# A hybrid attention layer on one core: modulation weights in long rows, and inverse roots spread by an identity matmul

## The chip, the cores and the metric

The kernel runs on one core of one Trainium2 chip. The metric is device time in microseconds: the median of several runs of the compiled program. The profile is of one further execution. Engines are named as the profile names them: PE (TensorE matmuls), PEld (its weight loads), DVE (VectorE), ACT (ScalarE), POOL (GpSimd), SP (SyncE, which issues the loads and stores).

## The reference

One layer of a diffusion backbone, depth 1, model width 1024, 1024 latent tokens and 256 context tokens, in float32. What matters here, cut:

```python
sh_a, sc_a, g_a, sh_f, sc_f, g_f = split(silu(c) @ w_ada + b_ada, 6)      # latent tokens
csh_a, csc_a, ...                = split(silu(c_ctx) @ w_ada + b_ada, 6)  # context tokens
h = rmsnorm(x) * (1 + sc_a) + sh_a
qa, ka, va, cq, ckv, krope = split(h @ w_in)          # 512, 512, 512, 256, 128, 32 columns
qb  = rmsnorm(cq, q_a_norm) @ w_q_up ; kvb = rmsnorm(ckv, kv_a_norm) @ w_kv_up
oa  = softmax(q1 k1) v - lam * softmax(q2 k2) v       # 4 differential heads of 2 x 64
oa  = rmsnorm(oa, diff_subln) * (1 - lam_init)
ob  = softmax(qb kb) vb                               # 8 latent heads
new = x + g_a * (concat(oa, ob) @ w_out)
h   = rmsnorm(new) * (1 + sc_f) + sh_f
out = rmsnorm(new + g_f * ((silu(h @ w_gate) * (h @ w_up)) @ w_ffn_out), final_norm)
```

An rmsnorm divides each token by the root of the mean of its squares. The modulation vectors (sh, sc, g) are products of one vector, silu(c) or silu(c_ctx), with columns of `w_ada` (1024 x 6144).

## The kernel before

Activations lie transposed: model columns on the 128 partitions, in 8 chunks k of 128, tokens along the free axis in slices of 512, 512 and 256 (`SLICES`). To keep float32 accuracy, most operands are split in a high and a low part of the rounded type fp32r (`split`: ACT copies the high part, DVE or POOL subtracts it), and a product is three matmuls, high by high, high by low, low by high. Plain f32 matmuls are used for small sums. A plain f32 matmul shows in the trace as two matmul instructions (two passes).

**First stage** (lines 446 to 621, order written out by hand for PE, ACT, DVE and POOL; SP issues loads in program order and waits there for a buffer to come free). The tokens x come in 8 loads of 640 KB, rows of 5 KB. ACT squares them, DVE adds the squares up (L541, L543), and `column_sums` (L416) gives the sum of each token with f32 matmuls of two columns. `inverse_rms` (L420, L421) makes the inverse root, tokens on the partitions. To multiply it into x it must lie along the free axis on every partition: `spread` (L423) writes the diagonal matrices identity times inverse, 128 x 128 for each 128 tokens, on DVE for the first slice and on POOL for the others (L426), and multiplies them by a matrix of ones (L427); ACT copies the result to `rstd`.

The modulation of chunk k needs two blocks of `w_ada` (1024 x 128 each, shift and scale), loaded by `load_ada` (L466, two loads of 512 KB in rows of 512 bytes; the tag `wa` has three buffers), split (`split_ada`; low parts on POOL and DVE, L479), multiplied by silu(c) and silu(c_ctx), both split too, four columns (`ada_part`, L506: 16 matmuls of 256 columns), copied to a row (`ada_row`, L510), turned to columns (L515) and added to the bias (`ada_columns`, L517). `modulate` (L524, L525, L528) scales, shifts and splits x to `hH` and `hL`. `group` (L600) then multiplies chunk k into seven PSUM banks for three blocks of `w_in` (cq, ckv): 14 matmuls for the high part, 7 for the low part. The products of chunk k + 1's modulation stand between them.

**Projections** (to about 345 us): the other blocks of `w_in`, rope, the low-rank norms (`low_stats`, `low_diag` L743, `low_norm` L759) and stores to DRAM; between them POOL sums the modulation rows of the later vectors (`mod_row`, L675 to L681). The first to execute are the key columns (`wk2`, L834).

**Attention** (to about 800 us): a list of operations, `attention_graph`, with engine, duration, dependencies and priority; a planner, `schedule`, orders them before the program is built. The norm of the differential heads is in it: `square`, `sums`, `mean`, `root`, `inverse_root`, `diagonal` (POOL, L1196), `spread` (PE, L1200), `apply` (DVE).

**Output projection, second norm, feed-forward, final norm**: `stat` (L1304) sums squares and writes the diagonals on DVE (L1316), `spread_stat` (L1319) multiplies them by ones (L1321). This occurs for each half of the tokens after its output projection, and in three parts at the end.

## Time and profile before

| | |
|---|---|
| runs, median of 3 | 1575.68 us (1570.89 to 1576.01) |
| profiled execution, its own time | 1571.2 us |
| its span, first to last instruction | 1569.3 us |
| PE busy, share of the span | 96% |
| DVE, ACT, POOL | 72%, 48%, 50% |

Busy time of PE is pipelined, a matmul's duration holds its way through the array, so two that follow each other overlap; what one costs in a stream is the distance between starts. Times in a trace are microseconds from the start of the span.

### The profile page before, as it was taken

What the parts mean: (1) busy time and instruction counts of PE and PEld (TensorE: products, weight loads), DVE (VectorE), ACT (ScalarE), POOL (GpSimd) and SP (SyncE); (2) the same over time, 40 slices, a digit from 0 to 9 for tenths busy, and PEclk for the clock granted to TensorE, in tenths of its full rate; (3) what the DMA queues carried; (4) which work ended last, traced back from release to release, by engine and by line L of the source; (5) the groups of instructions that cost most, each with busy time, mean ns of one, the idle gap of its engine ahead of it and who ended that gap; (6) DMA issues with size and microseconds to landing.
All of it is one profiled execution on the core that took longest, in us unless ns stands there. A gap on an engine that the chain in (4) does not pass through costs nothing.

```text
span 1569.3 us, 20682 instructions
## 1 busy us (share of the span) xinstructions
PE 1499.1 (96%) x7323; PEld 1210.4 (77%) x7323; DVE 1123.8 (72%) x1630; ACT 752.5 (48%) x1184; POOL 787.0 (50%) x547
## 2 busy tenths in 40 slices
PE   4899999989999999999999989999999999999997
PEld 2577888866777878888878767888888888888876
DVE  5758565569999879999854697655555555899883
ACT  5443321157777766777753454333333333444451
POOL 2437245526777847756511565755544441484221
PEclk8899999999999999999999989999999999999999
DMA  8426988596344434533146302322222224975633
GB/s 262 140 80 215 318 293 241 179 272 164 91 104 110 121 108 128 121 115 98 58 117 186 128 27 81 121 81 81 81 81 81 81 81 136 358 271 180 208 101 108
DMA packets 153922, 227.69 MB, mean 145 GB/s; under 512 B 11215, under 2 KB 80859, under 8 KB 153819
## 3 DMA queue, kind: packets, MB, share of 16 engines
q1 hardware_dynamic: 153547, 226.11, 46.7%
q8 instruction: 58, 0.95, 0.2%
q14 instruction: 45, 0.37, 0.1%
q10 hardware_dynamic: 272, 0.26, 0.0%
HBM read 172.53 MB, written 53.81 MB: 144 GB/s over the span
## 4 chain that ended last, share of the span: by engine, by line
PE 70%; DVE 10%; DMA 6%; POOL 5%; issue 3%; ACT 3%; SPq 1%; DVEq 0%; ACTq 0%; POOLq 0%
PE mm L1427 25%; PE mm L1715 10%; PE S L1056 10%; PE T L1118 6%; PE acc L1135 4%; PE acc L1140 3%; PE mm L1355 3%; PE mm L410 2%; PE ps L1355 1%; DMA wa<-in_w_ada_dram 1%; PE mm L600 1%; POOL sh L645 1%; POOL macc L681 1%; PE S L1355 1%; POOL e L1104 1%
## 5 line engine op out<-in xcount | busy, mean ns | idle before, releaser
L1056 PE MATMUL S<-kt,qt 128*128 128x512 f32 (+1 forms) x768 | 197.9, 362 | 10.5 <-ACT e L1090 8.7
L1090 ACT ACTIVATE e<-S,nm 128x1280 f32<-128x1280 f32 x128 | 170.3, 1331 | 46.4 <-DVE nm L1076 37.9
L1715 PE MATMUL mm<-block 128*128 128x512 f32 x792 | 179.7, 389 | 0.0
L1122 ACT ACTIVATE ph<-T 128x512 fp32r<-128x512 f32 x240 | 140.3, 597 | 81.9 <-PE T L1118 77.7
L1715 PEld LDWEIGHTS mm<-block 128*128 128x128 f32 x792 | 148.7, 188 | 30.8
L1072 DVE TENSOR_REDUCE nm<-S 128x1 f32<-128x1024 f32 x128 | 156.2, 1220 | 22.5 <-PE S L1056 21.1
L1126 DVE TENSOR_TENSOR pl<-T,ph 128x512 fp32r<-128x512 f32 x240 | 160.0, 682 | 15.8 <-ACT ph L1122 15.0
L1056 PEld LDWEIGHTS S<-kt,qt 128*128 128x128 f32 x768 | 131.8, 189 | 39.1 <-ACT e L1090 15.1
L1118 PE MATMUL T<-ident,e 128*128 128x128 f32 x960 | 140.4, 274 | 3.1 <-DVE pl L1126 1.7
L1110 POOL TENSOR_SCALAR e<-e,ls 128x1280 f32<-128x1280 f32 x64 | 88.0, 1376 | 102.6 <-DVE ls L1107 71.5
L1118 PEld LDWEIGHTS T<-ident,e 128*128 128x128 f32 x960 | 114.0, 141 | 32.1 <-DVE pl L1126 6.4
L1135 PE MATMUL acc<-ph,vt 128*128 128x512 f32 x320 | 120.9, 418 | 1.1 <-DVE otmp L1156 1.0
L1427 PE MATMUL mm<-fresh,wh 128*128 128x512 f32 x352 | 114.8, 406 | 3.4 <-DVE fresh L1580 3.3
L1427 PE MATMUL mm<-block,wh 128*128 128x512 f32 x352 | 112.2, 400 | 0.0
L1140 PE MATMUL acc<-pl,vt 128*128 128x512 f32 x240 | 104.6, 436 | 0.0
L1532 POOL TENSOR_TENSOR hd<-acc,v 128x512 f32<-128x512 f32 x22 | 29.7, 1349 | 149.4 <-DVE acc L1528 137.8
L344 ACT ACTIVATE wh<-wf 128x1024 fp32r<-128x1024 f32 (+1 forms) x51 | 52.2, 1025 | 103.4 <-issue 68.2
L1300 POOL TENSOR_TENSOR acc<-acc,sq 128x512 f32<-128x512 f32 x23 | 34.3, 1489 | 124.6 <-ACT sq L1298 124.0
L1104 POOL TENSOR_TENSOR e<-e,e 128x1280 f32<-128x1280 f32 x32 | 94.2, 2944 | 2.7
L410 PE MATMUL mm<-hH,wh 128*128 128x512 f32 (+1 forms) x256 | 95.2, 372 | 0.0
L410 PE MATMUL mm<-hH,wl 128*128 128x512 f32 (+1 forms) x256 | 94.0, 367 | 0.0
L410 PE MATMUL mm<-hL,wh 128*128 128x512 f32 (+1 forms) x256 | 93.8, 367 | 0.0
(357 smaller groups left out, 3613.3 us busy)
## 6 DMA issues: line engine op xcount, KB each, us to landing
wf<-in_w_ffn_in_dram SPq DMA_DIRECT2D x44, 512.0 KB, 3.7
hidD<-hd SPq DMA_DIRECT2D x44, 256.0 KB, 2.1
wh<-in_w_ffn_out_dram SPq DMA_DIRECT2D x21, 512.0 KB, 5.3
wl<-hidD SPq DMA_DIRECT2D x17, 512.0 KB, 5.7
wa<-in_w_ada_dram SPq DMA_DIRECT2D x16, 512.0 KB, 4.0
wa<-in_w_ada_dram SPq DMA_DIRECT2D x32, 256.0 KB, 3.7
qt<-QB SPq DMA_DIRECT2D x32, 256.0 KB, 4.7
qt<-QA SPq DMA_DIRECT2D x32, 256.0 KB, 4.9
```

The lines of the kernel that those rows point to most:

```text
L410: PE.matmul(ps, a(k), b(k), start=start and i == 0, stop=stop and i == n - 1)
L1056: m = PE.matmul(S[:, c0:c0 + w], q, k[:, k0:k0 + w], start=s == 0, stop=s == len(job) - 1)
L1072: on_banks(DVE.tensor_reduce(self.stats(n)[0][:, i:i + 1], sl, AX.X, ALU.max, negate=True), BANKS[i], DVE)
L1090: m = ACT.activation(e, S[:, i * NT:(i + 1) * NT], AF.Exp, bias=self.s[n][0][:, i:i + 1], accum_out=total)
L1104: POOL.tensor_tensor(self.e[n, 0], self.e[n, 0], self.e[n, 1], ALU.add)
L1118: PE.transpose(self.T[c][:, b * P:(b + 1) * P], e[:, kc * P:(kc + 1) * P], ident)
L1122: ACT.activation(self.ph[c], self.T[c], AF.Copy)
L1126: DVE.tensor_tensor(self.pl[c], self.T[c], f32(self.ph[c]), ALU.subtract)
L1135: PE.matmul(self.acc[u, qh, j], vt[:, kc, v], self.ph[c], start=kc == 0 and i == 0, stop=False)
L1140: PE.matmul(self.acc[u, qh, j], self.kv[u][1][:, kc, v], self.pl[c], start=False, stop=kc == 9)
L1427: PE.matmul(ps, a[:, k, :], b, start=k == 0 and i == 0, stop=k == 3 and i == 2)
L1715: PE.matmul(ps[d], w[:, sl], x[:, t0:t0 + n], start=first and c == 0 and i == 0, stop=c == NH - 1 and i == 2, skip_group_check=not first)
```

## The change

It has four parts.

1. *Layout.* The first 2048 columns of `w_ada` become an input of their own, `w_first`, so arranged that each load of `load_ada` reads rows of 4 KB; `w_ada` keeps the rest. `w_in` and `w_out` are stored by blocks of 128 columns, which also gives rows of 4 KB.
2. *Order and buffers of the first stage.* Chunk 0's weights are loaded after two blocks of x, two of the three `w_in` blocks between the others; chunk 2's weights and the key columns are loaded later. High and low parts of the modulation weights get a buffer for each half. All low parts are made on DVE. The loop over chunks is rearranged: modulation of chunk k + 1 and weights of chunk k + 2 are worked on beside chunk k's products.
3. *Three chunks unsplit.* The weights of chunks 0, 1 and 2 aren't split; `ada_whole` multiplies them in f32, 16 matmuls of 128 columns. For the other five, `ada_parts` has 32 matmuls of 128 columns in the place of 16 of 256.
4. *Spreading.* In all norms the diagonals go: `spread` multiplies, for each 128 tokens, the column of inverses, repeated 128 times by a stride of zero, by the identity. In attention the operation `diagonal` leaves the planner's list.

```diff
     def spread(h, qh, root):
-        d = op("Pool", 1.4, [root] + spreads[-1:], "diagonal", h, qh)
-        s = after("T", op("PE", 0.86, [d] + T[-2], "spread", h, qh, kind="diagonal"))
+        s = after("T", op("PE", 0.86, [root] + T[-2], "spread", h, qh, kind="diagonal"))
         a = op("DVE", 0.66, [s], "apply", h, qh, kind="diagonal")
         T.append([a])
         spreads.append(s)
...
-    def spread(ps, rs, dg, n, eng):
+    def spread(ps, rs, n):
 
         for t in range(n // P):
-            eng.tensor_scalar(dg[:, t * P:(t + 1) * P], ident, rs[:, t:t + 1], 1.0, ALU.mult, ALU.mult)
-        PE.matmul(ps[:, :n], ones, dg[:, :n], start=True, stop=True)
+            PE.matmul(ps[:, t * P:(t + 1) * P], rs[:, t:t + 1].to_broadcast([P, P]), ident, start=True, stop=True)
 
     def win_cols(c0, m):
-        return w_in.rearrange("(k p) c -> p k c", p=P)[:, :, c0:c0 + m]
+
+        return w_in[:, c0 * KD:(c0 + m) * KD].rearrange("p (k c) -> p k c", k=KD)
...
-    for k in range(KD):
+
+    def part_tile(tag):
+        return sp.tile([P, KD, P], F32R, tag=tag, name=tag, bufs=4)
+
+    def room(tag, n):
+        return f32(part_tile(tag)).rearrange("p a b -> p (a b)")[:, 0:n]
+
+    pieces = slice(0, 512), slice(512, NT)
+    acc = [room("wal", 512), room("wal", 768)]
+    sqs = [room("wah", 512), room("wah", 768)]
+    small = room("wal", 512)
+    smalls = small[0:60, 384:512]
+    lp = small[:, 0:256].rearrange("p (a b) -> p a b", b=64)
+    pr = small[:, 256:384].rearrange("p (a b) -> p a b", b=64)
+
+    def load_x(k):
         dma(x[:, k, :], xT[k * P:(k + 1) * P, :])
-        if k == 1:
-            dma(smalls, vecs.rearrange("(c p) -> c p", p=P))
-            dma(lp, diff_lambda.rearrange("a b -> (a b)").partition_broadcast(P))
 
     def load_ada(k):
 
         was = []
         for i in range(2):
             was.append(sp.tile([P, KD, P], F32, tag="wa", name="wa", bufs=3))
-            dma(was[i], w_ada.rearrange("(r p) c -> p r c", p=P)[:, :, i * D + k * P:i * D + (k + 1) * P])
+            dma(was[i].rearrange("p r c -> p (r c)"), w_first[k][:, i * D:(i + 1) * D])
         return was
...
-    def split_ada(wa, eng, eng2=None, between=None):
-        wah, wal = ada_tiles()
+    def split_ada(wa, between=None):
+        wah, wal = ([part_tile(tag) for i in range(2)] for tag in ("wah", "wal"))
         for i in range(2):
-            ACT.activation(wah[:, i], wa[i], AF.Copy)
+            ACT.activation(wah[i], wa[i], AF.Copy)
         for i in range(2):
-            if i and between:
+            DVE.tensor_tensor(wal[i], wa[i], f32(wah[i]), ALU.subtract)
+            if i == 0 and between:
                 between()
-            (i and eng2 or eng).tensor_tensor(wal[:, i], wa[i], f32(wah[:, i]), ALU.subtract)
         return wah, wal
...
     st.enter_context(tc.manual_schedule(engines=ENGINES))
+    load_x(0)
+    load_x(1)
     was = [load_ada(0)]
-    mixw = [fetch_w(mix_cols(i), P) for i in range(2)]
+    dma(smalls, vecs.rearrange("(c p) -> c p", p=P))
+    dma(lp, diff_lambda.rearrange("a b -> (a b)").partition_broadcast(P))
+    mixw = []
+    for k in range(2, KD, 2):
+        load_x(k)
+        load_x(k + 1)
+        if k < KD - 2:
+            mixw.append(fetch_w(mix_cols(k // 2 - 1), P))
     was.append(load_ada(1))
     wkr = sp.tile([P, KD, 32], F32, name="wkr")
-    dma(wkr, win_cols(1920, 32))
-    was.append(load_ada(2))
...
+    def ada_whole(k):
+
+        for i in range(2):
+            for r in range(KD):
+                PE.matmul(adp[0:2, i * P:(i + 1) * P], cv[:, r, :], was[k][i][:, r, :], start=r == 0, stop=r == KD - 1)
...
+    def ada_parts(w):
+
+        for i in range(2):
+            for n, p in enumerate(w):
+                for r in range(KD):
+                    PE.matmul(adp[0:4, i * P:(i + 1) * P], c4[:, r, :], p[i][:, r, :], start=r + n == 0, stop=r == KD - 1 and n == 1)
+
+    def ada_row(m):
+        row = sp.tile([4, 256], F32, tag="row", name="row", bufs=1)[0:m]
+        ACT.activation(row, adp[0:m, 0:256], AF.Copy)
+        return row, sel if m == 4 else ident[0:2, 0:2]
+
+    def ada_turn(row, sel):
         for i in range(2):
             PE.matmul(adp[:, 256 + 2 * i:258 + 2 * i], row[:, i * P:(i + 1) * P], sel, start=True, stop=True)
+
+    def ada_columns(k):
         for i in range(2):
             DVE.tensor_scalar(modA[:, 8 * i + k, :], adp[:, 256 + 2 * i:258 + 2 * i], bT[:, 8 * i + k:8 * i + k + 1],
                               float(i), ALU.add, ALU.add)
...
-    def modulate(k):
+    def scale(k):
         for j, (t0, n) in ((0, (0, 512)), (0, (512, 512)), (1, (1024, 256))):
             sl = slice(t0, t0 + n)
             sh, sc, t = modA[:, k, j:j + 1], modA[:, 8 + k, j:j + 1], x[:, k, sl]
             DVE.scalar_tensor_tensor(t, t, sc, rstd[:, sl], ALU.mult, ALU.mult)
             ACT.activation(hH[:, k, sl], t, AF.Identity, bias=sh)
+
+    def shift_low(k):
...
     for k in range(KD):
-        for sq, sl in zip(sqs, halves):
-            sq = sq if k else acc[:, sl]
+        for sq, to, sl in zip(sqs, acc, pieces):
+            sq = sq if k else to
             ACT.activation(sq, x[:, k, sl], AF.Square)
             if k:
-                DVE.tensor_tensor(acc[:, sl], acc[:, sl], sq, ALU.add)
+                DVE.tensor_tensor(to, to, sq, ALU.add)
...
+        if k == 3:
+            ada_whole(0)
+        if k == 6:
+            row = ada_row(2)
+        if k in (5, 6):
+            split(*mixw[k - 5])
         if k >= KD - 3:
 
             for t0 in (0, 512):
                 PE.matmul(warm, ones, x[:, k, t0:t0 + 512], start=True, stop=True)
-    column_sums(msp, acc, NT)
-    adp = mm_tile()
-    wads = [ada_tiles()]
-    wah, wal = wads[0]
-    for i in range(2):
-        ACT.activation(wah[:, i], was[0][i], AF.Copy)
-    ACT.activation(mixw[0][0], mixw[0][2], AF.Copy)
+    ada_turn(*row)
+    rstd = sp.tile([P, NT], F32, name="rstd")
     rsc = sp.tile([P, 10], F32, name="rsc")
-    DVE.tensor_tensor(wal[:, 0], was[0][0], f32(wah[:, 0]), ALU.subtract)
+    msp = mm_tile()
+    column_sums(msp, acc[0], 512)
+    column_sums(msp[:, 8:], acc[1], 768)
     inverse_rms(rsc, msp[:, 0:20], D)
-    ACT.activation(mixw[1][0], mixw[1][2], AF.Copy)
-    ada_part(wads[0], 0)
-    rstd = sp.tile([P, NT], F32, name="rstd")
+    ada_columns(0)
     for i, (t0, n) in enumerate(SLICES):
         rb = mm_tile()
-        spread(rb, rsc[:, t0 // P:], dg[:, t0:t0 + n], n, POOL if i else DVE)
-        if i == 0:
-            DVE.tensor_tensor(wal[:, 1], was[0][1], f32(wah[:, 1]), ALU.subtract)
-            for w in mixw:
-                DVE.tensor_tensor(w[1], w[2], f32(w[0]), ALU.subtract)
+        spread(rb, rsc[:, t0 // P:], n)
         ACT.activation(rstd[:, t0:t0 + n], rb[:, :n], AF.Copy)
-    ada_part(wads[0], 1)
-
 
...
-    ada_columns(0, ada_row())
-    wads.append(split_ada(was[1], POOL, DVE, lambda: modulate(0)))
+    scale(0)
     mixw.append(fetch_w(mix_cols(2), P))
+    was.append(load_ada(2))
+    dma(wkr, win_cols(1920, 32))
+    ada_whole(1)
+    row = ada_row(2)
+    shift_low(0)
     split(*mixw[2])
-    wads.append(split_ada(was[2], POOL, DVE))
+    wads = {}
     wk2 = const.tile([P, KD, 64], F32R, name="wk2")
 
-    def group(k, part):
-        for ps, (b, i) in zip(lows, low):
+    def group(k, part, which=low):
+        for ps, (b, i) in zip(lows[low.index(which[0]):], which):
             t0, n = SLICES[i]
             x_ = h_parts(t0, n)[part]
             for w in range(2 - part):
                 PE.matmul(ps[:, :n], mixw[b][w][:, k, :], x_(k), start=k == 0 and part == 0 and w == 0,
                           stop=k == KD - 1 and part == 1)
 
+    group(0, 0, low[:5])
+    ada_turn(*row)
     for k in range(KD):
-        if k == 0:
-            group(0, 0)
-        if k + 1 < KD:
-            for i in range(2):
-                ada_part(wads[k + 1], i)
-            row = ada_row()
         if k + 3 < KD:
             was.append(load_ada(k + 3))
-            wads.append(split_ada(was[k + 3], POOL, DVE if k % 2 else None))
-        if k == 3:
+        if k + 1 < KD:
+            ada_columns(k + 1)
+            scale(k + 1)
+        low_part = (lambda: shift_low(k + 1)) if k + 1 < KD else None
+        if k + 3 < KD:
+            wads[k + 3] = split_ada(was[k + 3], low_part)
+        elif low_part:
+            low_part()
+        if k == 4:
             split(wk2[:, :, 0:32], wk2[:, :, 32:64], wkr)
-        group(k, 1 if k == 0 else 0)
-        if k + 1 < KD:
-            ada_columns(k + 1, row)
-            modulate(k + 1)
         if k:
-            group(k, 1)
+            group(k, 0)
+        else:
+            group(0, 1, low[:5])
+            group(0, 0, low[5:])
+        if k + 2 < KD:
+            if k:
+                ada_parts(wads[k + 2])
+            else:
+                ada_whole(2)
+            row = ada_row(4 if k else 2)
+        group(k, 1, low if k else low[5:])
+        if k + 2 < KD:
+            ada_turn(*row)
     st.close()
...
-    def low_diag(i):
-        t0, n = SLICES[i]
-        dgs[0, i] = bp.tile([P, 512], F32, tag="dg0", name="dg0", bufs=1)
-        diag(dgs[0, i], rskv[:, t0 // P:], n, DVE)
-        if t0 < NL:
-            dgs[1, i] = bp.tile([P, 512], F32, tag="dg1", name="dg1", bufs=1)
-            diag(dgs[1, i], rsq[:, t0 // P:], n, DVE)
-
...
-            PE.matmul(ps[:, :n], ones, dgs[min(bs[0], 1), i][:, :n], start=True, stop=True)
+            spread(ps, (rsq if bs[0] else rskv)[:, t0 // P:], n)
...
-        if i < 2:
-            got.insert(-3, lambda: low_diag(i + 1))
...
-            low_diag(0)
...
-        def diagonal(self, h, qh):
-            self.dg = at.tile([P, 512], F32, tag="sq", name="dg", bufs=1)
-            for t in range(4):
-                r = self.ms[:, h * 8 + qh * 4 + t:h * 8 + qh * 4 + t + 1]
-                POOL.tensor_scalar(self.dg[:, t * P:(t + 1) * P], ident, r, 1.0, ALU.mult, ALU.mult)
-
         def spread(self, h, qh):
             self.T["s"] = lps.tile([P, 512], F32, tag="T", name="T", bufs=2)
-            PE.matmul(self.T["s"], ones, self.dg, start=True, stop=True)
+            spread(self.T["s"], self.ms[:, h * 8 + qh * 4:h * 8 + qh * 4 + 4], 512)
...
-        dg = tmp_tile("dg", 1)[:, :n]
-        for t in range(n // P):
-            eng.tensor_scalar(dg[:, t * P:(t + 1) * P], ident, rs[:, t:t + 1], 1.0, ALU.mult, ALU.mult)
-        return dg
-
-    def spread_stat(dg, n):
+        return rs
+
+    def spread_stat(rs, n):
         rb = mm_tile()[:, :n]
-        PE.matmul(rb, ones, dg, start=True, stop=True)
+        spread(rb, rs, n)
         return rb
...
+
+    def by_chunk(w):
+
+        return w.reshape(KD, P, -1).transpose(1, 0, 2).reshape(P, -1)
...
-        ("w_ada", a["w_ada"][0]),
+        ("w_first", a["w_ada"][0][:, :2 * D].reshape(KD, P, 2, KD, P).transpose(3, 1, 2, 0, 4).reshape(KD, P, 2 * D)),
+        ("w_ada", a["w_ada"][0][:, 2 * D:]),
...
-        ("w_in", a["w_in"][0]),
+        ("w_in", np.concatenate([by_chunk(a["w_in"][0][:, c:c + P]) for c in range(0, 1952, P)], axis=1)),
...
-        ("w_out", a["w_out"][0]),
+        ("w_out", np.stack([by_chunk(a["w_out"][0][:, c:c + P]).reshape(P, KD, P) for c in range(0, D, P)])),
```

## Rows read from the trace of the kernel before

**Rows 1.** The page, part 1: busy time of the engines.
```profile
PE 1499.1 (96%) x7323; PEld 1210.4 (77%) x7323; DVE 1123.8 (72%) x1630; ACT 752.5 (48%) x1184; POOL 787.0 (50%) x547
```

**Rows 2.** Stretches: length; PE, PEld, DVE, ACT, POOL busy; granted clock; DMA share; GB/s.
```profile
48.00:50.00 2.00, 2.00 (x12) 1.17 (x10) 0.11 (x1) 0.00 (x0) 0.00 (x0) 0.50 0.84 232
...
200.00:250.00 50.00, 50.00 (x263) 42.53 (x262) 28.93 (x52) 10.96 (x21) 18.60 (x15) 1.00 0.88 281
900.00:920.00 20.00, 15.34 (x53) 10.43 (x54) 19.73 (x26) 10.49 (x16) 11.93 (x9) 0.91 0.09 27
```

**Rows 3.** Timeline, 20 to 45: start, us, engine, line, operation, [idle before, releaser].
```profile
25.98 0.22 DVE L421 RECIPROCAL rsc<-rsc 128x10 f32<-128x10 f32 x1 [2.02 <-ACT rsc L420]
...
26.41 5.29 POOL L426 TENSOR_SCALAR room<-ident,rsc 128x128 f32<-128x128 f32 x6 [24.96 <-DVE rsc L421]
...
31.06 2.93 PE L427 MATMUL mm<-room,ones 128*128 128x512 f32 x4 [1.59 <-POOL room L426]
...
40.21 0.79 PE L600 MATMUL mm<-hH,wh 128*128 128x512 f32 x1 [4.07 <-ACT hH L525]
...
42.46 1.22 DVE L479 TENSOR_TENSOR wal<-wa,wah 128x1024 fp32r<-128x1024 f32 x1
```

**Rows 4.** Timeline, the last chunks of the first stage, 95 to 109.
```profile
95.31 1.81 DVE L524 SCALAR_TENSOR_TENSOR x<-x,modA,rstd 128x512 f32<-128x512 f32 x3
...
96.38 1.10 PE L506 MATMUL mm<-wah,c 128*4 128x256 f32 x8
...
97.52 1.68 DVE L528 SCALAR_TENSOR_TENSOR hL<-x,modA,hH 128x1024 fp32r<-128x1024 f32 x2 [0.39 <-ACT hH L525]
...
98.25 0.39 PE L600 MATMUL mm<-hH,wh 128*128 128x512 f32 x1
...
101.37 0.60 PE L515 MATMUL mm<-sel,row 4*128 4x2 f32 x4
...
107.45 1.67 PE L600 MATMUL mm<-hL,wh 128*128 128x512 f32 x7
```

**Rows 5.** Stretches: long rows of x (14 to 16), 512-byte rows (22 to 24).
```profile
14.00:16.00 2.00, 0.29 (x1) 0.29 (x2) 1.70 (x3) 1.73 (x3) 0.00 (x0) 1.00 1.00 415
22.00:24.00 2.00, 2.00 (x11) 1.21 (x9) 1.85 (x2) 1.66 (x2) 0.00 (x0) 1.00 1.16 290
```

**Rows 6.** Load issued at 7.2 (KB, us to landing); timeline, last addition of squares.
```profile
x<-in_xT_dram SPq DMA_DIRECT2D x1, 640.0 KB, 11.6
...
21.80 0.82 DVE L543 TENSOR_TENSOR room<-room,lpr 128x640 f32<-128x640 f32 x1
```

**Rows 7.** Timeline, 47 to 50.
```profile
47.03 0.51 PE L600 MATMUL mm<-hH,wl 128*128 128x512 f32 x1 [2.31 <-DVE wl L347]
...
47.84 1.88 PE L506 MATMUL mm<-wah,c 128*4 128x256 f32 x8
```

**Rows 8.** The chain that ended last: start, us, what; projections, attention, end.
```profile
113.14 1.26 POOL macc L681
...
353.25 0.87 PE T L1118 x8
...
1533.19 0.86 PE mm L1321 x2
```

**Rows 9.** Tile wa: ScalarE's copies (ns min/median/max) and its loads to landing.
```profile
L475 ACT ACTIVATE wah<-wa x14: 1038/1042/1047, 35.4 to 84.7; 128x1024 fp32r<-128x1024 f32 x14
...
DMA to landing us min/median/max: 3.1/3.9/13.1
```

**Rows 10.** Timeline, second norm, 895 to 904.
```profile
895.63 5.88 DVE L1316 TENSOR_SCALAR dg<-ident,rs 128x128 f32<-128x128 f32 x4
...
901.57 2.08 PE L1321 MATMUL mm<-dg,ones 128*128 128x512 f32 x2 [3.85 <-DVE dg L1316]
```

**Rows 11.** Timeline, final norm.
```profile
1561.13 0.69 DVE L1316 TENSOR_SCALAR dg<-ident,rs 128x128 f32<-128x128 f32 x2
```

**Rows 12.** Line L1196, attention's diagonals: ns min/median/max, first and last start.
```profile
L1196 POOL TENSOR_SCALAR dg<-ident,ms x32: 371/373/379, 579.2 to 651.1; 128x128 f32<-128x128 f32 x32
```

More of the change, by code (lines that the diff above doesn't have):

```diff
@@ L310, in tile_hybrid_diffattn_mla_dit_layer @@
     cc: bass.AP,
+    w_first: bass.AP,
     w_ada: bass.AP,
@@ L502, in tile_hybrid_diffattn_mla_dit_layer @@
         DVE.tensor_tensor(sel[:, i:i + 1], ident[0:4, i:i + 1], ident[0:4, i + 2:i + 3], ALU.add)
-    def ada_part(w, i):
-        for r in range(KD):
-            PE.matmul(adp[0:4, 0:256], c4[:, r, :], w[i][:, :, r, :], start=r == 0 and i == 0, stop=r == KD - 1 and i == 1)
-    def ada_row():
-        row = sp.tile([4, 256], F32, tag="row", name="row", bufs=1)
-        ACT.activation(row, adp[0:4, 0:256], AF.Copy)
-        return row
-    def ada_columns(k, row):
+    def ada_whole(k):
[12 more added lines that the diff above has]
+    def ada_turn(row, sel):
         for i in range(2):
             PE.matmul(adp[:, 256 + 2 * i:258 + 2 * i], row[:, i * P:(i + 1) * P], sel, start=True, stop=True)
+    def ada_columns(k):
         for i in range(2):
@@ L1313, in stat @@
         inverse_rms(rs, ps[:, 0:2 * (n // P)], D)
-        dg = tmp_tile("dg", 1)[:, :n]
-        for t in range(n // P):
-            eng.tensor_scalar(dg[:, t * P:(t + 1) * P], ident, rs[:, t:t + 1], 1.0, ALU.mult, ALU.mult)
-        return dg
-    def spread_stat(dg, n):
+        return rs
+    def spread_stat(rs, n):
         rb = mm_tile()[:, :n]
-        PE.matmul(rb, ones, dg, start=True, stop=True)
+        spread(rb, rs, n)
         return rb
@@ L1335, in shift2, with norm2_first @@
         ACT.activation(nl[k, qh], nl[k, qh], AF.Identity, bias=modF[:, 8 + k:9 + k])
-    def norm2_first(dg):
-        rb = spread_stat(dg, 512)
+    def norm2_first(rs):
+        rb = spread_stat(rs, 512)
         for k in range(KD):
@@ L1399, in tile_hybrid_diffattn_mla_dit_layer @@
         if d == 0:
-            dg = stat(0, 512, DVE)
+            rs = stat(0, 512)
         if d == 1:
-            norm2_first(dg)
+            norm2_first(rs)
     kept = [0]
@@ L1832, in tile_hybrid_diffattn_mla_dit_layer @@
         if c == AT[2]:
-            dg = stat(0, 256, DVE)
+            rs = stat(0, 256)
         if c == AT[3]:
-            rb = [spread_stat(dg, 256) for _ in range(2)]
+            rb = [spread_stat(rs, 256) for _ in range(2)]
         chunk_product("p4", c, ps, (3,), 256)
     square(KD - 1, 256, add_to(KD - 1, 0, ps[3], 256))
-    dg = stat(256, 256, DVE)
-    last = [spread_stat(dg, 256) for _ in range(2)]
+    rs = stat(256, 256)
+    last = [spread_stat(rs, 256) for _ in range(2)]
     final(0, 0, 256, rb, SHARED[0])
```

32 lines of the change are left out of this document (10 added, 22 removed).

## Prediction

> **What bounds the kernel now.** I read the page first [rows 1]: TensorE is busy for 96% of the span, so a gain must come from a stretch where it is not. The table of stretches shows the projections full (50.00 of 50 us) and the second norm, 900 to 920, not [rows 2]. The timeline names a third hole, in the first stage [rows 3]. The inverse root is there at 26.2 (25.98 and 0.22), the first projection matmul starts at 40.21, after waiting 4.07 us for modulated tokens: 14.0 us in which GpSimd writes diagonals (5.29 us) and TensorE spreads the last of them from 31.06. From there the stage is near TensorE's own pace and ends at 109.1 [rows 4]; four key matmuls of 0.23 us are pulled ahead of that, so 108.2.
>
> **First stage, up to the inverse.** Loads come in another order: two blocks of x, chunk 0's weights, the small vectors, then x mixed with two projection weights. Ahead of the last x block stand four more loads of 512 KB, 2.1 MB. Long rows (x, 5 KB) moved at 415 GB/s, rows of 512 bytes at 290 [rows 5]; the new rows have 4 KB, so I take 415: 5.0 us. About 1 us of this I strike out, since before some bytes of the weights moved between the last x. The last x was issued at about 7.2 and landed 11.6 us later, at 18.8, but VectorE's last addition ended only at 22.6 [rows 6]. After, x lands at 22.8; its squares and additions in two pieces (512 and 768 columns, together 2.5 us by the 640-column addition of 0.82), 12 passes of column sums at 0.107 and the root end at 27.3: 1.1 us later. If 4 KB rows ran at 290, 2.2 us more.
>
> Chunk 0's product (16 f32 matmuls) and the splits of two projection weights run while x is awaited; this idle time covers them. Without it, the product would cost 3.4 us, as chunk 1's does. The small vectors land some 2.5 us later; their first reader that counts is chunk 0's column step at 27. The key weights and chunk 2's loads move behind the third projection weight on SP's queue and wait there, with chunk 3's behind them, for chunk 1's first buffer, free at about 32: chunk 2 is there by 36, just ahead of its product, and the key weights are wanted five chunks later. Nothing is charged.
>
> **From the inverse to the first projection.** The diagonals go. A 512-column f32 matmul is two passes, 0.86 us [rows 8], so 0.107 for 128 columns; the new one is four 128-column matmuls, each with a weight load. The nearest rows with a load per 128 columns are transposes, 8 in 0.87 us [rows 8]: the same price. Unhidden loads would double it; I take the row, since it has this shape. Ten such matmuls cost 2.2 us at full clock, 4.3 at half; I take 3.2. Then come chunk 1's unsplit weights: 16 f32 matmuls, 32 passes, 3.4 us, and 0.4 for the hand-over. TensorE reaches its first projection matmul at 34.3 instead of 40.2; tokens are scaled by about 32.
>
> **The chunks.** Eight of 4.6 us (3.0 from 98.25 to the turn, 1.6 for the low part), six turns of 0.6 [rows 4], chunk 2's unsplit product 3.4. Five chunks stay split, and their product changes from 16 matmuls of 256 columns (8 in 1.10, so 1.9 per chunk) to 32 of 128. No row has a rounded-f32 matmul so narrow. From below it is the same number of columns, 1.9; from above two f32 passes, 0.215 each, 6.9 per chunk; single-pass transposes give 3.5. I take 2.5, nearest the row that has the same operands, with something for twice the instructions. The Trainium skill (TensorE: Matmul & The Clock Gate, section Back-to-back issue gap) gives a stream of weight loads and 128-column matmuls about 81 ns for each: by that estimate 2.6 per chunk, and the sum would be half a microsecond worse; no row here shows it. Total 36.8 + 3.6 + 3.4 + 12.5 = 56.3.
>
> The low parts of the weights move from GpSimd to VectorE: per chunk 1.8 + 1.7 + 2 x 1.2 + 0.3 = 6.2 us [rows 3, 4], below TensorE's 7.7, so VectorE stays off the path.
>
> A new wait: the last load of chunk 3 takes the buffer of chunk 2's first half, free only when TensorE has read it. ScalarE's copy of that load stands ahead of its copy of chunk 2's row; TensorE's turn waits for that row, with chunk 1's projections queued behind it. Load 3.3 (the shortest was 3.1), copy 1.04 [rows 9], row and hand-over 0.9, less 2.2 us of work that TensorE still has: 3.1 us idle. After a wait of 2.31 us the granted clock was 0.50, the 1.2 GHz level, and eight narrow matmuls took 1.88 instead of 1.10 [rows 2, 4, 7]: 2 us more. End 34.3 + 56.3 + 5.1 = 95.7 against 108.2: **12.5 us gained**. What follows is TensorE's own stream [rows 2], so it carries.
>
> **The other norms.** In the second norm VectorE writes the diagonals in 5.88 us, and TensorE waits 3.85 us for them [rows 10]; VectorE is full there [rows 2]. I take 3.7 (0 if the split queued behind them comes no earlier, 5.9 if all of it is path). At the end the spread follows the reciprocal without 0.7 us of diagonals [rows 11]. In attention GpSimd's diagonals, and in the low-rank norms VectorE's, hide under TensorE: nothing; uncovered, attention's alone, 32 of 0.37, would be some 12 us [rows 12]. The planner's order there can move by an operation or two, a microsecond either way. Long rows of the input and output projections: nothing, no matmul waits for them. Twenty spreads at +0.01: 0.2 lost.
>
> **Sum.** 12.5 + 3.7 + 0.7 - 0.2 = 16.7 off the profiled execution's 1571.2: 1554.5. That execution lies 4.5 below the median of the three runs (1575.68), which stand at 1571 and 1576; I add 1.5 and predict **1556**.
>
> **Rivals**, on the same basis.
> *Narrow matmuls dear* (slower side). The 128-column matmuls cost two f32 passes, 6.9 per chunk: 5 x 4.4 = 22 us more, 1578. It makes a loss of the gain from 5.9 us per chunk on, 0.18 per matmul. For it: no row has this shape, and it is the price of the f32 kind. Against: at 256 and 512 columns this kind goes in one pass. 0.13.
> *Hidden.* The stage is shorter, but what follows is paced by the modulation rows; the 12.5 are lost, 1568.5. For it: the chain of waits runs through GpSimd's additions there [rows 8]. Against: TensorE is full all the while. 0.10.
> *Half clock.* With 2 or 4 weight columns TensorE does not hold its clock: the spread 1, chunk 1 3.4 and the first chunk 4 us dearer, 1564. For it: the clock at 48 [rows 2]. Against: later it stays full with such matmuls in between. The Trainium skill (TensorE: Matmul & The Clock Gate, section Why this matters for your kernels) warns of waits between bursts of matmuls; the row agrees. 0.15.
> *No new stall.* The load is early enough, narrow matmuls cost 1.9 and all 5.9 us of the diagonals count: 5.1 + 3 + 2.2 less, 1546. 0.10.
> The forecast has 0.52.
>
> **Numbers.** 1556 is the likeliest; its own range is 1550 to 1562. The whole range takes in the early case, the half clock and the hidden case: 1544 to 1571, leaving out the dear matmuls and the ends, 0.2. A difference below 0.3%, 4.7 us, can't be told from none. Forecast, half clock, early case and half of the hidden one lie beyond it: faster 0.80; the other half and some of the dear case: same 0.11; slower 0.09.
>
> **What would show it.** The first projection matmul near 34 (right) or still near 40; 32 matmuls of a split chunk in 2.5 us; 3 us without TensorE before chunk 2's turn, with ScalarE waiting for a load; the last low matmul near 96 and a full TensorE after it; no wait before the spread near 885. I am wrong if the narrow matmuls take 0.2 us each, or if TensorE idles in the projections.

## The result and the profile after

| | before | after |
|---|---|---|
| median of the runs timed side by side | 1575.85 us (4 runs) | 1558.63 us (4 runs) |
| ratio, 95% interval | | 0.9889 (0.9864 to 0.9915) |
| the same again, beside the last experiment | 1571.54 us (11 runs) | 1558.78 us (6 runs) |
| ratio, 95% interval | | 0.9918 (0.9894 to 0.9942) |
| profiled execution, its span | 1569.3 us | 1556.9 us |

Forecast were 1556 us (1544 to 1571) and a gain of 16.7 on the profiled execution. The time came out 2.6 us above the forecast; both intervals lie below 1. The gain between the two profiled executions is 12.4. Where it arises is read from the starts of the same matmuls in both traces:

| place | before | after | earlier by |
|---|---|---|---|
| first projection matmul (L600; L620) | 40.21 | 37.37 | 2.8 |
| last low projection matmul ends | 109.12 | 96.90 | 12.2 |
| last key matmul ends (after it none of the order differs) | 126.41 | 115.09 | 11.3 |
| first score matmul of attention | 322.26 | 311.29 | 11.0 |
| first feed-forward matmul (`block`, `wh`) | 890.15 | 879.70 | 10.4 |
| second norm over (first `block`, `sh`) | 944.11 | 932.60 | 11.5 |
| first matmul of the last output (`block`, `Y`) | 1519.27 | 1507.74 | 11.5 |
| span | 1569.3 | 1556.9 | 12.4 |

So the first stage gives 11.3, projections and attention lose 0.9, the second norm gives 1.1 and the tail 0.9. The first part of the page of the changed kernel answers to [rows 1]:

```profile
PE 1501.0 (96%) x7565; PEld 1226.2 (79%) x7565; DVE 1101.7 (71%) x1596; ACT 746.6 (48%) x1178; POOL 742.7 (48%) x499
```

TensorE has 242 instructions more and is as busy as before; GpSimd is busy 44 us less. The timeline of its first stage (start, us, engine, line, operation, idle before and releaser) answers to [rows 3, 4, 7]:

```profile
26.72 2.39 PE L416 MATMUL mm<-ones,wal 128*128 128x2 f32 x20
...
29.45 0.22 DVE L421 RECIPROCAL rsc<-rsc 128x10 f32<-128x10 f32 x1 [2.25 <-ACT rsc L420]
...
29.72 4.13 PE L426 MATMUL mm<-ident,rsc 128*128 128x128 f32 x20 [0.61 <-DVE rsc L421]
33.78 3.66 PE L520 MATMUL mm<-wa,cT 128*2 128x128 f32 x32
37.37 0.51 PE L620 MATMUL mm<-hH,wh 128*128 128x512 f32 x1
...
47.83 1.06 ACT L480 ACTIVATE wah<-wa 128x1024 fp32r<-128x1024 f32 x1 [3.64 <-DMA wa<-in_w_first_dram]
48.79 0.36 ACT L531 ACTIVATE row<-mm 2x256 f32<-2x256 f32 x1
...
49.20 0.60 PE L536 MATMUL mm<-ident,row 2*128 2x2 f32 x4 [2.52 <-ACT row L531]
...
54.41 0.64 PE L527 MATMUL mm<-wah,c 128*4 128x128 f32 x8
54.89 0.64 PE L527 MATMUL mm<-wal,c 128*4 128x128 f32 x8
...
95.23 1.67 PE L620 MATMUL mm<-hL,wh 128*128 128x512 f32 x7
```

The inverse root is there at 29.7, 3.5 us later than before; spread and chunk 1's product follow without a gap. Until 47.83 ScalarE waits 3.64 us for a load, and the copy of chunk 2's row stands behind it: TensorE waits 2.52. From there to the end of the stage it waits for nothing; eight narrow matmuls start every 0.48 us.

Only 2.8 of the 12.2 us by which the stage ends earlier come ahead of the first projection matmul; 9.4 come behind it. There the kernel before waits at eight places, 8.2 us in all: the 2.31 of [rows 7] and others like these of its timeline:

```profile
59.41 0.50 PE L600 MATMUL mm<-hH,wh 128*128 128x512 f32 x1 [2.03 <-ACT hH L525]
...
75.25 0.50 PE L600 MATMUL mm<-hH,wh 128*128 128x512 f32 x1 [0.81 <-ACT hH L525]
...
91.46 0.51 PE L600 MATMUL mm<-hH,wh 128*128 128x512 f32 x1 [0.85 <-ACT hH L525]
```

The changed kernel waits 2.5 us there. With 5.7 us of waits less, four key matmuls (0.9 us) moved behind the stage and a granted clock of 0.97 instead of 0.94 over it, the 9.4 us are made up to within some tenths.

In the second norm (timeline, answers to [rows 10]) the wait for diagonals is gone, and several others stand in its place, three of them here (`block,wl` and `fresh,sh`):

```profile
887.09 1.05 PE L426 MATMUL mm<-ident,rs 128*128 128x128 f32 x8
...
887.60 1.15 ACT L344 ACTIVATE wh<-wf 128x512 fp32r<-128x512 f32 x2 [1.74 <-DMA wf<-in_w_ffn_in_dram]
...
888.26 3.55 DVE L347 TENSOR_TENSOR wl<-wf,wh 128x512 fp32r<-128x512 f32 x2 [3.13 <-ACT wh L344]
...
890.18 0.50 PE L1432 MATMUL mm<-block,wl 128*128 128x512 f32 x1 [1.16 <-DVE wl L347]
...
896.76 0.50 PE L1432 MATMUL mm<-fresh,sh 128*128 128x512 f32 x1 [1.18 <-ACT fresh L1581]
...
898.38 0.50 PE L1432 MATMUL mm<-fresh,sh 128*128 128x512 f32 x1 [1.12 <-DVE fresh L1585]
```

VectorE, freed of 5.88 us of diagonals, stands idle for 3.13 us instead: next in its queue is the low part of a weight whose load lands only now, and the scaling of the tokens is behind that. Over the whole norm TensorE stands idle for 10.2 us, before the change for 9.3: the wait has moved on rather than gone, and that the norm is 1.06 shorter all the same goes with a granted clock of 0.94 there instead of 0.87.

### The profile page after: what moved, and what is told of

The parts are those of the page before. It is cut to its first block, busy times and chain, and to the rows that moved or that the text cites. A ratio compares the mean times of both kernels' runs of the same rounds, so it can differ in the third digit from the quotient of the medians.

```text
span 1556.9 us, 21067 instructions
## 1 busy us (share of the span) xinstructions
PE 1501.0 (96%) x7565; PEld 1226.2 (79%) x7565; DVE 1101.7 (71%) x1596; ACT 746.6 (48%) x1178; POOL 742.7 (48%) x499
## 3 DMA queue, kind: packets, MB, share of 16 engines
q1 hardware_dynamic: 110539, 226.11, 46.1%
## 4 chain that ended last, share of the span: by engine, by line
PE 78%; DVE 8%; DMA 6%; issue 3%; ACT 3%; POOL 2%; SPq 0%; DVEq 0%; ACTq 0%; POOLq 0%
PE mm L1432 25%; PE mm L1720 10%; PE S L1070 10%; PE mm L410 6%; PE T L1132 6%; PE acc L1149 4%; PE acc L1154 3%; PE mm L620 3%; PE mm L1360 3%; PE ps L1360 1%; PE S L1360 1%; POOL e L1118 1%; ACT e L1104 1%; DMA wf<-hidD 1%; DVE nm L1086 1%
## 5 line engine op out<-in xcount | busy, mean ns | idle before, releaser
L1070 PE MATMUL S<-kt,qt 128*128 128x512 f32 (+1 forms) x768 | 198.1, 363 | 10.2 <-ACT e L1104 9.0
L1537 POOL TENSOR_TENSOR hd<-acc,v 128x512 f32<-128x512 f32 x22 | 29.7, 1350 | 148.2 <-DVE acc L1533 136.7
```

Source lines behind the costliest of these rows:

```text
L1070: m = PE.matmul(S[:, c0:c0 + w], q, k[:, k0:k0 + w], start=s == 0, stop=s == len(job) - 1)
```

## The experiments

Executions of one kernel differ by up to 11 us. Much of this lies at the end: from the first `Y` matmul on, the thirteen profiles taken after the one of before need 45.2 to 51.4 us. So the profiles are compared by stretches. "Stage" is from the first projection matmul to the end of the last low one, "norm" from the first feed-forward matmul to the first `block`, `sh`; all in us.

| kernel | first projection matmul | stage | norm | median of its runs (of before, same chip) |
|---|---|---|---|---|
| before | 40.21 | 68.9 | 53.96 | 1575.85 |
| changed | 37.37 | 59.5 | 52.90 | 1558.63 (1575.85) |
| spread_only | 34.95 | 70.4 | 52.90 | 1561.25 (1575.50) |
| no_rows | 39.68 | 60.1 | 52.89 | 1565.19, one run |
| row_first | 36.77 | 57.8 | 52.92 | 1557.49, one run |
| row_all | 38.63 | 55.3 | 52.91 | 1559.97, one run |
| late_split | 37.80 | 59.7 | 50.85 | 1553.54, one run |
| late_split2 | 36.84 | 59.7 | 52.92 | 1560.78, one run |
| lean_start | 37.36 | 59.8 | 52.91 | 1557.84, one run |
| all_whole | 36.92 | 64.4 | 52.89 | 1562.68, one run |
| split_2 | 37.84 | 56.0 | 52.89 | 1552.47, one run |
| early_spread | 38.01 | 59.6 | 52.07 | 1560.04, one run |
| rows_and_spread | 36.92 | 55.3 | 52.07 | 1554.54 (1571.54) |
| change_again | 38.40 | 59.7 | 52.88 | 1558.78 (1571.54) |

**spread_only: part 4 alone on the kernel before.**

```diff
-        spread(rb, rsc[:, t0 // P:], dg[:, t0:t0 + n], n, POOL if i else DVE)
+        spread(rb, rsc[:, t0 // P:], n)
...
-        dg = tmp_tile("dg", 1)[:, :n]
-        for t in range(n // P):
-            eng.tensor_scalar(dg[:, t * P:(t + 1) * P], ident, rs[:, t:t + 1], 1.0, ALU.mult, ALU.mult)
-        return dg
+        return rs
```

> The kernel before with part 4 of the change alone: all norms spread by the identity, layout, order and splits of the first stage as before. Theory (the norms are a small part): in the first stage the spread no longer waits for diagonals, but the four-column product of chunk 0 with its low parts and the turn still stand between it and the first projection matmul, so that this comes 1 to 2.5 us earlier (40.2 to about 38.5) and no more; the second norm gives about 1 us and the tail 0.9, as in the changed kernel. Together 3 to 4 us, some 1567.5 profiled. Rival 1 (the prediction's term): the second norm gives 3.7, together 6. Rival 2: GpSimd's diagonals are the hole itself; the first projection matmul then comes at 36 or earlier and the part is worth 6 to 8 us.

Its timeline, and then its stretch 35 to 52 (length; PE, PEld, DVE, ACT, POOL busy; granted clock; DMA share; GB/s):

```profile
26.46 2.39 PE L425 MATMUL mm<-ident,rsc 128*128 128x128 f32 x20
...
30.27 0.60 PE L513 MATMUL mm<-sel,row 4*128 4x2 f32 x4 [0.46 <-ACT row L508]
34.95 0.79 PE L598 MATMUL mm<-hH,wh 128*128 128x512 f32 x1 [4.08 <-ACT hH L523]
```

```profile
35.00:52.00 17.00, 14.26 (x57) 9.50 (x57) 9.88 (x10) 6.80 (x9) 6.38 (x3) 0.62 0.48 136
```

The second rival was right at the start: the first projection matmul comes 5.3 us earlier, so the diagonals were most of the hole. The stage then runs 1.5 us longer, with the clock granted at 0.62 over 17 us after the 4.08 us wait, and ends at 105.35 instead of 109.12. So of the 12.2 us by which the changed kernel ends the stage earlier, part 4 makes 3.8; 6.7 us of waits inside the stage stay, so it is parts 1 to 3 that close them, and the layout few of them, since no_rows (below), which lacks it, waits 3.1 there. What order and unsplit chunks give apart from each other no run shows. The norm gives the same 1.06 as in the changed kernel. The run times do not separate part 4 from the whole change: its median lies 14.2 us below the kernel before, ratio 0.9918 (0.9892 to 0.9944), the same as in the second timing of the whole change. The profiled execution, the slowest of its four (1566.73), lies only 4.4 us below that of before in its span. That parts 1 to 3 add something rests on the profiles: at the first feed-forward matmul spread_only is 4.1 us earlier than before, the changed kernel 10.4.

**no_rows: the changed kernel without long rows.**

```diff
-            dma(was[i].rearrange("p r c -> p (r c)"), w_first[k][:, i * D:(i + 1) * D])
+            dma(was[i], w_first.rearrange("(r p) c -> p r c", p=P)[:, :, i * D + k * P:i * D + (k + 1) * P])
...
-        return w_in[:, c0 * KD:(c0 + m) * KD].rearrange("p (k c) -> p k c", k=KD)
+        return w_in.rearrange("(k p) c -> p k c", p=P)[:, :, c0:c0 + m]
```

> The changed kernel with the old layout of the modulation weights and of the input projection (rows of 512 bytes), all else as changed. Theory: the loads between the blocks of x take longer, x comes later by up to 2.2 us (2.1 MB at 290 instead of 415 GB/s) and the late load of chunk 3 by about 0.5; first projection matmul at 38 to 39.6 instead of 37.4, last low matmul of the stage at 98 to 99.6 instead of 96.9. Rival: loads are waited for at one place only, the rows are worth nothing; stage end within 0.5 us of 96.9.

About as the theory had it: the first projection matmul comes 2.3 us later, 1.05 beyond the latest of six profiles of the changed order (below), and the stage ends 2.9 later, each 0.1 to 0.2 past the theory's upper bound. The stretch 14 to 24 of the changed kernel and of this one, and two rows of this one's timeline:

```profile
14.00:24.00 10.00, 8.16 (x26) 3.67 (x25) 9.18 (x18) 9.12 (x14) 0.00 (x0) 0.83 1.02 417
```

```profile
14.00:24.00 10.00, 7.37 (x26) 3.59 (x24) 8.61 (x17) 7.88 (x12) 0.00 (x0) 0.83 1.06 371
```

```profile
27.06 1.55 DVE L563 TENSOR_TENSOR wal<-wal,wah 128x512 f32<-128x512 f32 x2
...
50.69 1.06 ACT L479 ACTIVATE wah<-wa 128x1024 fp32r<-128x1024 f32 x1 [4.17 <-DMA wa<-in_w_first_dram]
```

The DMA engines are as busy with both, and move 417 or 371 GB/s. VectorE's last addition ends at 28.6 here and at 27.0 to 27.3 in the six profiles, so x does come later. ScalarE's wait for the late load grows from 3.64 to 4.17 us, TensorE's behind it from 2.5 to 3.1. Another 1.1 us of the 2.9 are spread and product (4.64 and 4.29 us instead of 4.13 and 3.66), which scatter with the clock among the six as well.

**row_first and row_all: the row ahead of a late load.** The first for chunk 2 alone, the second, row_all, for every chunk (`high_ada` copies a high half, `low_ada` subtracts for a low one); the edit of row_all, cut:

```diff
+        if k + 2 in wads:
+            low_ada(k + 2, 1)
         if k + 3 < KD:
-            wads[k + 3] = split_ada(was[k + 3], low_part)
+            wads[k + 3] = [[part_tile(tag) for i in range(2)] for tag in ("wah", "wal")]
+            high_ada(k + 3, 0)
+            low_ada(k + 3, 0)
...
             row = ada_row(4 if k else 2)
+            if k + 3 < KD:
+                high_ada(k + 3, 1)
```

> The changed kernel with ScalarE's copy of chunk 3's second half behind the copy of chunk 2's row, and its low part behind chunk 2's scaling on VectorE. Theory: the 2.5 us without TensorE before chunk 2's turn were ScalarE's queue behind a late load, and the half clock after it, about 2 us, came of that wait; both go, the stage ends at about 92.4 instead of 96.9. Rival 1: the late load is then waited for at chunk 3's product, whose low parts come too late; 1 to 2 us gained. Rival 2: the clock falls there anyway; 2.5 gained.

> As the run with the row ahead, but in every chunk: ScalarE copies the row between the two high halves, VectorE's second low half follows the next chunk's scaling. Theory: with chunk 2's row ahead the wait came back as 0.7 us for the rows of chunks 3 to 5, since ScalarE's two copies still stood ahead of them; with every row ahead no turn waits, and from the first projection matmul to the last low one it takes 55 us (59.5 changed, 57.8 with chunk 2's row alone). Rival: loads or VectorE's later low halves are waited for instead: 57 us or more.

Timeline of row_first at the turns of chunks 2 and 3:

```profile
46.01 0.60 PE L536 MATMUL mm<-ident,row 2*128 2x2 f32 x4
...
54.05 0.60 PE L536 MATMUL mm<-sel,row 4*128 4x2 f32 x4 [0.73 <-ACT row L531]
```

The wait is gone at 46, but 1.7 of the 4.5 us came out. That is the size of its first rival, but at another place: TensorE now waits for the rows of later chunks, up to 0.8 at a time and 2.2 in all, behind ScalarE's two copies. With every row ahead the stage takes 55.3, as expected. The stretch 46 to 52, of the changed kernel and of row_all:

```profile
46.00:52.00 6.00, 3.48 (x15) 2.71 (x15) 4.08 (x8) 2.10 (x4) 0.00 (x0) 0.88 0.79 264
```

```profile
46.00:52.00 6.00, 6.00 (x41) 4.56 (x40) 5.60 (x9) 3.07 (x5) 0.00 (x0) 1.00 0.77 236
```

**late_split, late_split2 and lean_start: why the inverse is late.** late_split moves the two projection weights' splits and chunk 0's row with its turn behind the root, late_split2 the splits alone; lean_start is late_split2 without the matmuls by ones (the last blocks of x times a matrix of ones, their results unread). The edit of lean_start, cut:

```diff
-        if k in (5, 6):
-            split(*mixw[k - 5])
-        if k >= KD - 3:
-
-            for t0 in (0, 512):
-                PE.matmul(warm, ones, x[:, k, t0:t0 + 512], start=True, stop=True)
...
     ada_columns(0)
+    split(*mixw[0])
+    split(*mixw[1])
```

> The changed kernel with the splits of the two projection weights and chunk 0's row moved from between the last squares to behind the root. Theory: the inverse comes at 29.7 instead of the forecast 27.3 because 2.4 us of these copies and subtractions stand in the queues of ScalarE and VectorE ahead of the last squares and additions; moved, the inverse is there at about 27.3, the first projection matmul at 35 instead of 37.4, and the stage ends 2 to 2.4 us earlier, near 94.7. Rival 1: x itself is late, the inverse stays at 29.2 or later and the moved splits only delay the scaling: stage end 96.9 or later. Rival 2: the inverse comes earlier, but VectorE's subtractions ahead of the scaling and the third projection weight, loaded later, eat it: gain under 1 us.

> The changed kernel with only the splits of the two projection weights behind the inverse; chunk 0's row and turn stay where they are. Theory: in the first trial the inverse did come 1.35 us earlier (28.3 after 29.7), and TensorE gave it back with the turn that then stood ahead of the spread, and with more of chunk 1's product at half clock; now the spread begins at about 28.5 and the first projection matmul comes at about 36.2 instead of 37.4, the stage ends near 95.8. Rival: TensorE's clock is low until the same moment whatever comes earlier: first projection matmul at 37 or later.

> The changed kernel with the two projection weights split behind the inverse and without the twelve matmul passes by ones that keep TensorE busy on the last blocks of x. Theory: the inverse comes late (29.4 to 31 in six profiles of the same stage instead of the forecast 27.3) for two reasons of like size: VectorE's last addition ends at 26.2 to 27.2, and TensorE works at those passes until 25.3 to 27.5 and only then begins the column sums; in the runs that moved one of the two, the other held the end. With both gone the inverse is there at 28.2 or earlier and the first projection matmul at about 36.5, with spread and chunk 1's product still mostly at half clock. Rival: without those passes TensorE's clock stays low longer, and spread and product cost 1.5 us or more extra; first projection matmul at 37.5 or later.

Timeline of late_split:

```profile
23.56 0.63 ACT L562 ACTIVATE wah<-x 128x512 f32<-128x512 f32 x1 [0.22 <-DMA x<-in_xT_dram]
...
25.23 0.96 DVE L564 TENSOR_TENSOR wal<-wal,wah 128x768 f32<-128x768 f32 x1 [0.31 <-ACT wah L562]
...
28.10 0.22 DVE L421 RECIPROCAL rsc<-rsc 128x10 f32<-128x10 f32 x1 [1.90 <-ACT rsc L420]
...
29.31 4.64 PE L426 MATMUL mm<-ident,rsc 128*128 128x128 f32 x20
33.88 4.00 PE L520 MATMUL mm<-wa,cT 128*2 128x128 f32 x32
```

Timeline of lean_start, and then its stretch 26 to 28:

```profile
24.94 4.42 PE L416 MATMUL mm<-ones,wal 128*128 128x2 f32 x20 [0.32 <-DVE wal L563]
29.98 3.87 PE L426 MATMUL mm<-ident,rsc 128*128 128x128 f32 x20 [0.61 <-DVE rsc L421]
```

```profile
26.00:28.00 2.00, 2.00 (x11) 2.00 (x11) 0.15 (x1) 0.00 (x0) 0.00 (x0) 0.50 0.29 105
```

My theories fell here. In late_split the additions end at 26.2 instead of 27.2 and the inverse comes 1.35 us earlier, but the first projection matmul does not: the turn stands ahead of the spread, which takes 4.64, and the product 4.00 instead of 3.66. In lean_start the column sums take 4.42 us at clock 0.50 instead of the 2.39 of late_split2, from which it differs by the matmuls by ones alone, and the inverse is at 29.9. So these buy two microseconds of column sums. With one and the same order up to that point the first projection matmul lies between 36.77 and 38.63 in six profiles (changed, row_first, row_all, early_spread, rows_and_spread, change_again), depending on where in this stretch the granted clock is low: the sums begin between 26.1 and 28.0 behind the matmuls by ones, and the spread takes 3.67 to 4.64. The 36.84 of late_split2 and the 37.36 of lean_start lie inside that, so no gain is shown.

**all_whole and split_2: more chunks unsplit, or fewer.**

```diff
-            if k:
-                ada_parts(wads[k + 2])
-            else:
-                ada_whole(2)
-            row = ada_row(4 if k else 2)
+            ada_whole(k + 2)
+            row = ada_row(2)
```

For split_2, on row_all:

```diff
-    wads = {}
+    wads = {2: split_ada(was[2])}
...
+            ada_parts(wads[k + 2])
```

> The changed kernel with all eight chunks unsplit (f32 product of 3.66 us in place of 1.92 for chunks 3 to 7), their high and low copies gone, and six buffers for the loads in the room of those copies. Theory: after the first projection matmul TensorE's own stream sets the pace; five chunks cost 1.74 more each, 8.7, and the wait with its half clock, 4.5, goes with ScalarE's copies: from the first projection matmul to the last low one 63.7 us instead of 59.5. Rival: ScalarE's and VectorE's copies hold the pace as much as TensorE; 59 us or less, and splitting is not worth its work.

> The run with every row ahead, but with chunk 2 split as the later chunks are. Theory: chunk 2's f32 product costs TensorE 1.74 more than a split one, but splitting it puts 2.1 us of copies on ScalarE and 2.45 of subtractions on VectorE ahead of chunk 1's scaling, where both are behind TensorE; nothing is gained, from the first projection matmul to the last low one it takes 55 to 57.5 us (55.3 unsplit), with a wait of 1 to 2 us before chunk 2's turn. Rival: TensorE's stream is all that counts: 53.6.

Timeline of all_whole, and TensorE's waits of split_2 from 30 to 110 (us, times, longest):

```profile
49.93 3.66 PE L520 MATMUL mm<-wa,cT 128*2 128x128 f32 x32
```

```profile
PE mm L536 <- ACT row L531: 1.1, 1, 1.1
...
PE mm L527 <- DVE wal L627: 0.6, 1, 0.6
PE mm L527 <- DVE modA L540: 0.4, 1, 0.4
```

With all chunks unsplit TensorE waits for nothing and the stage takes 64.4, 9.1 more than row_all, which waits for nothing either (five products at 1.74 make 8.7): it is TensorE's stream that sets the pace, and splitting pays from chunk 3 on. With chunk 2 split, TensorE's 1.74 us come back as 2.1 us of waits: 56.0 against 55.3. Its low total comes from later stretches: from the first `Y` matmul on it needs 46.1 us, row_all 51.4.

**early_spread: the second norm.**

```diff
+        rb = spread_stat(rs, 512)
+        for k in range(2):
+            scale2(k, 1, rb)
         first[1].first(True)
         first[0].p2(False)
-        rb = spread_stat(rs, 512)
...
-        run(4, lambda k: (scale2(k, 1, rb), shift2(k, 1)),
+        run(4, lambda k: (k > 1 and scale2(k, 1, rb), shift2(k, 1)),
```

> The changed kernel with the second norm's spread one product earlier on TensorE, and two of the eight scalings of tokens ahead of the next weights' low parts on VectorE. Theory: in the second norm the diagonals' 5.88 us gave only 1.06 because VectorE then stands 3.1 us idle behind a weight load (its low part is next in the queue, the scalings behind it); two scalings of 0.66 go into that idle time. From the first feed-forward matmul to the block that ends the stretch: 52.9 us become 51 to 51.6. Rival: VectorE's and ScalarE's work behind it sets the pace from another operation on, or TensorE's wait for the inverse eats it: 52.4 or more.

Its timeline:

```profile
886.61 1.41 DVE L1337 SCALAR_TENSOR_TENSOR block<-block,scF,mm 128x512 f32<-128x512 f32 x2 [1.25 <-PE mm L426]
888.35 3.71 DVE L347 TENSOR_TENSOR wl<-wf,wh 128x512 fp32r<-128x512 f32 x2 [0.33 <-ACT wh L344]
```

The scalings do go into the idle time, and VectorE's wait for the copy falls from 3.13 to 0.33. The first block of new tokens (`fresh`, `sh`) is multiplied 1.25 us earlier, counted from the first feed-forward matmul; 0.83 of it is left at the end of the stretch. That is between theory and rival: the mechanism is shown, its worth was put too high.

**rows_and_spread and change_again.** Both edits that gained, and the changed kernel beside them.

> The changed kernel with both edits that gained in a profile: every row ahead of ScalarE's second copy, and the second norm's earlier spread. Theory: both are stretches in which TensorE was short of work, so they add: 4.2 us (59.5 to 55.3 in the first stage) and 0.8 (52.9 to 52.1 in the second norm), 5.0 us or 0.3% below the changed kernel timed beside it. Rival: the end of the kernel, which differs by up to 5 us from one execution to another, hides it: within 2 us of the changed kernel.

> The changed kernel itself, timed again beside the run with both edits. Theory: 1555 to 1560 us as before, and the first stage's end at 95 to 98.5 us, since its start depends on when TensorE's clock rises. Rival: the first timing was a lucky one, 1563 or more.

Stage 55.3 and norm 52.07: both gains are there together. The medians differ by 4.2 us, 1554.54 against 1558.78, for an expected 5.0; against the kernel before the ratio is 0.9890 (0.9873 to 0.9907), and the changed kernel's interval, 0.9894 to 0.9942, overlaps it. So the profiles show the gain, and the times agree with it without settling it. The changed kernel came out as expected, its stage end at 98.09 included. One source of the scatter is TensorE's wait near the end, of the changed kernel and of rows_and_spread:

```profile
PE mm L1318 <- DVE res L1735: 2.1, 1, 2.1
```

```profile
PE mm L1329 <- DVE res L1748: 2.6, 1, 2.6
```

In change_again and late_split it does not occur; there the stretch from the first `Y` matmul to the last takes 36.0 and 35.7 us instead of 39.6 and 40.1.

## Why the prediction was right, step by step

- **The hole, and that it closes.** Right. The spread waits only for the inverse; spread_only shows 5.3 us at the first projection matmul from this part alone. The reading that the rest of the stage was "near TensorE's own pace" was wrong: 8.2 us of waits stood there. The sum for the chunks counted TensorE's work only and so left them out without saying why; that came true but for the one new stall. By spread_only, which keeps 6.7 us of them, parts 1 to 3 closed them.
- **Inverse at 27.3.** Wrong by 2.4 us: 29.7. The step that failed counted x's last squares, additions and 12 passes of sums as if nothing else were queued on those engines. In late_split ScalarE's wait for x ends at 23.6, not 22.8. In the changed kernel the splits that "this idle time covers" push the last addition from 26.2 to 27.2, and TensorE is at its matmuls by ones and chunk 0's turn until 26.7 and only then starts on 20 passes of sums, 2.39 us, where the forecast had the last 12 passes of them left, 1.3 us.
- **Spread 3.2, chunk 1's product 3.4, hand-over 0.4.** Measured 4.13 and 3.66, then the projection at once. The price per 128 columns at full clock was right, 20 passes in 2.39 in spread_only (2.2 forecast); the changed kernel grants 0.57 during the spread, so the upper bound of 4.3 holds.
- **Narrow matmuls 2.5 per chunk.** 1.92, the lower bound: 32 at 0.060. Over five chunks 2.9 us cheaper than forecast, which by luck makes up for most of the 3.1 us by which the first projection matmul is late. The rival of dear matmuls is refuted. The Trainium skill (TensorE: Matmul & The Clock Gate, section Back-to-back issue gap) gives about 81 ns for a weight load with a 128-column matmul; here a pair takes 60, with four-column weights, and the measurement decides.
- **The new stall, 3.1 and 2 at half clock.** Right in place and cause: 2.52 waited, the clock 0.88 from 46 to 52 and 0.87 from 52 to 60. row_all, which takes it away and leaves the loads, gains 4.2, so the half clock costs 1.7.
- **The chunks 56.3.** Without any wait, in row_all, and with narrow matmuls at 1.92 they take 55.3, where the forecast's terms give 53.4. Seven turns stand in them, not six (chunk 1's, too, comes behind the first projection matmul, at 39.65), and a chunk takes about 0.15 more than 4.6.
- **Stage end 95.7, 12.5 gained.** 96.9 and, by the last key matmul, 11.3; the first projection matmul is 3.1 late and the chunks take 1.9 more, the narrow matmuls save 2.9 and the stall 0.9. *Hidden* is refuted: ten of these microseconds are still there at the first feed-forward matmul. *Half clock* came about for the spread and hardly for chunk 1: about 1 us of its 8.
- **Long rows of the input projection at nothing, of the modulation weights about 2.** no_rows: 2.9 for both in one profile, of which 1.1 can be the scatter of the clock at the stage's start.
- **Second norm 3.7.** This term failed; 1.06 measured, within 0.02 in ten profiles; only late_split has 50.85. There VectorE's four subtractions from 923.16 on (L1583) need 2.5 us from first start to last end, in the changed kernel (L1585, from 922.49) 5.8, while GpSimd's product beside them takes 3.41 instead of 1.65; why the one or the other is held up no run shows. The step took TensorE's wait before the spread for the path. Its lower bound named the reason ("if the split queued behind them comes no earlier"): the copy that waits for the weight load starts 7.6 us after the first feed-forward matmul before the change, 7.9 after it and 7.7 in early_spread, whatever VectorE does, and early_spread shows that the idle time left there can be used.
- **Tail 0.7, other norms nothing.** 0.9; projections and attention lost 0.9, which no run explains; attention alone, to the first feed-forward matmul, takes 568.3 to 571.2 us in the thirteen later profiles and took 567.9 before.
- **Sum.** 16.7 forecast, 12.4 between the profiles, 12.8 between the medians of the second timing and 17.2 of the first. The forecast of 1556 is nearer to 1558.6 than its sum deserves: it put 1.5 us on top for an execution that lay 4.5 below its median. Of the 4.3 us that the sum has too much, 2.6 are the second norm, 1.2 the first stage and the rest projections and attention.

## What to carry to other kernels

When a wait on the path is removed, ask for each engine what is next in its queue and when that operation's input lands: here the diagonals' 5.88 us became 1.06, since the next operation in its queue, behind a weight load, could start only 3 us after VectorE was free. Put a small copy that TensorE waits for ahead of a large one that waits for a load; that was worth 4.2 us of stage, a third of what the whole change gives between the profiles. Spreading a column by an identity matmul needs no diagonals from another engine, and its price is that of the passes at the clock that TensorE has at that point: 2.39 us for 20 in spread_only, 3.67 to 4.64 in the changed order. And test the smallest part alone: by run times part 4 cannot be told from the whole change, and only the stretches of the profiles show what the rest adds.

## What the runs showed of the hardware

- Matmuls of 128 columns in fp32r with four weight columns go at 0.060 us, half of the 256-column ones (eight start over 0.93 us before the change, 0.116 each).
- The same 20 spread passes were granted different clocks. Right behind half of chunk 0's modulation product (eight matmuls of 256 columns) they took 2.39 us at 1.00 (spread_only). Behind two-column sums and 0.61 us of waiting the changed kernel shows 1.00 up to 29.7 and 0.57 for the spread; which of the two brought the clock down no run shows:

```profile
26.00:29.70 3.70, 3.11 (x25) 2.82 (x24) 1.46 (x5) 0.27 (x1) 0.00 (x0) 1.00 0.91 355
29.70:33.70 4.00, 3.98 (x20) 3.94 (x20) 0.92 (x3) 1.09 (x2) 0.00 (x0) 0.57 0.03 8
```

- Matmuls by ones whose results nobody reads shorten the 20 sum passes after them: 2.39 us with them (late_split2), 4.42 without (lean_start). In the six profiles of the changed order the sums take 2.39 to 3.01.
